# Separate PSUM banks in gate/up, and ScalarE reading queries, keys and diagonal blocks beside the inverse

## The chip, the cores and the metric

The kernel runs on one core of a Trainium2 chip. The metric is the device time of one execution in microseconds (us), the median of several runs. The engines are named as in the profile: PE is TensorE's matmuls and PEld its weight loads, DVE is VectorE, ACT is ScalarE, POOL is GpSimd; SPq and ACTq are the DMA issues in the queues of SyncE and ScalarE.

## The reference, cut to what matters

One layer of a decoder over 1024 tokens of 1024 features, all in float32. A combined projection feeds two groups of four heads: a gated delta rule in chunks of 64 tokens and a differential attention. Their outputs go through one output projection, and then through a SwiGLU block with 2816 hidden features. The parts that the change touches:

```python
# gated delta rule, per head and chunk of 64 tokens
L = jnp.where(strict, jnp.einsum('nbhcd,nbhsd->nbhcs', k_beta, k) * decay, 0.0)
A = L + jnp.eye(CHUNK, dtype=f32)
sol = lax.linalg.triangular_solve(A, rhs, left_side=True, lower=True, unit_diagonal=True)
q = l2norm(q.astype(f32)) * (Dk ** -0.5)
...
# the feed-forward block
gate, up = jnp.split(h @ w_gate_up[l], 2, axis=-1)
x = x + (jax.nn.silu(gate) * up) @ w_down[l]
```

## The kernel before

**Numbers.** A float32 product is made of three matmuls in a rounded 32-bit format: each operand is split into a high part (suffix `_h`) and the remainder (`_l`), and high x high, low x high and high x low are summed in PSUM (`mm3`, L144 to L146). So every projection result that is used again as an operand has to be read out of PSUM as a high part and a low part.

**PSUM.** All eight banks are taken: two tiles `big` of two banks each, two tiles `sm` and two tiles `fl` of one bank each. A dependency is tracked by tile: a matmul into one half of a `big` tile waits for every earlier instruction that reads the other half.

**Order.** A scheduler orders the instructions of each engine ahead of time; the program text gives it priorities and dependencies. Each engine then runs its own list in order, and a waiting instruction holds all that stand behind it, DMA issues included.

**The stage of the delta rule.** A loop over four heads (L463 to L486) makes keys and queries by projection, convolution and SiLU, sums their squares, and forms on PE the products K K^T and K Q^T in blocks of 128 tokens. DVE scales these with the decay into `At` (L482, tile `ak`) and `intra` (L485, tile `dec`). GpSimd then raises the sums of squares to a power (L489 `nk`, L490 `rqs`), and DVE scales `rqs` (L491), which is used only after the inverse. Then the diagonal 32x32 blocks of `At` are inverted: DVE transposes them with four instructions, one per group of 32 partitions, straight out of `At` (L502 to L504); 31 elimination steps of two small DVE instructions each follow (L506 to L511), and two more transposes (L514, L515). The products that go on from the inverse begin with L594 on PE.

**Beside the inverse** PE computes queries and keys of the attention's first two heads (`qk_dense`, in the order Q0, K0, Q1, K1; the halves n=0 and n=1 of the tokens share one `big` tile) and the value projections `v_dense`. For each half ACT writes the scaled high part out of PSUM (L535), and DVE reads PSUM again and subtracts it for the low part (L536). These parts lie in tiles `cv`, of which there are four buffers, and are sent to DRAM by DMAs issued on ACT's queue (L544, L545 for queries; L547, L548 for keys). The weights of the next projection are split by ACT (L151, the high part) and DVE (L153, the low part) or GpSimd (L157).

**The gate/up stage.** `gate_up(f)` runs for f = 1 to 21 (f = 0 is written out by itself, L1289 to L1321) and makes one 128-feature slice of gate and up for all tokens by a Strassen-like scheme: seven products of 12 matmuls each (`product`, L1200), in the order A11, S2, S3, S1, A12, S4, A22. `banks()` gives it four accumulators: `pa` is a tile `sm`, `pb` a tile `fl`, and `pc` and `pd` are the two halves of one `big` tile. S3 and A22 accumulate in `pc`, S1 and S4 in `pd`. DVE adds partial results (L1213) straight out of PSUM after each product: `u3` out of `pc` after S3, `tu` out of `pd` after S1, `tg` out of `pd` after S4, `tu` out of `pc` after A22. Between them DVE also forms the sums of raw weights for a later slice (L1168) and low parts (L1105). Raw gate and up weights come by DMA on SyncE's queue (L1156, L1158). The down projection follows.

Of the kernel before, what the change touches and what calls it, by code (L numbers as in the profile page):

```python
# [16 lines left out]
P = 128  # L17
# [51 lines left out]
def decoder_kernel(ctx: ExitStack, tc: tile.TileContext, a: dict, out: bass.AP):  # L69
# [392 lines left out]

    for h in range(H):  # L463
# [9 lines left out]
        for half in range(2):  # L473
            kk = sm()
            kq = sm()
            for jj in range(4):
                js = slice((half * 4 + jj) * P, (half * 4 + jj + 1) * P)
                nc.tensor.matmul(kk[:, jj * P:(jj + 1) * P], lhsT=KT[h][:, js], rhs=KT[h][:, js], start=True, stop=True)
                nc.tensor.matmul(kq[:, jj * P:(jj + 1) * P], lhsT=KT[h][:, js], rhs=QT[h][:, js], start=True, stop=True)
            b0 = h * 8 + half * 4  # L480
            for jj in range(4):
                nc.vector.scalar_tensor_tensor(out=At[:, b0 + jj, :], in0=kk[:, jj * P:(jj + 1) * P],  # L482
                                               scalar=brk_f[:, b0 + jj:b0 + jj + 1], in1=dec[:, b0 + jj, :],
                                               op0=ALU.mult, op1=ALU.mult)
            nc.vector.tensor_tensor(out=dec[:, b0:b0 + 4, :], in0=kq.rearrange("p (a b) -> p a b", a=4),  # L485
                                    in1=dec[:, b0:b0 + 4, :], op=ALU.mult)  # L486
    intra = dec
# [3 lines left out]
    nc.vector.tensor_scalar(out=rqs, in0=rqs, scalar1=DK ** -0.5, scalar2=None, op0=ALU.mult)  # L491
# [10 lines left out]
    for q in range(4):  # L502
        qs = slice(32 * q, 32 * q + 32)
        nc.vector.transpose(out=B[qs], in_=At[qs, :, qs].rearrange("s h c -> s c h"))  # L504
# [12 lines left out]
    def qk_dense(h, is_q, ps_of, mid=None):  # L517
# [6 lines left out]
        for n in range(2):  # L524
# [9 lines left out]
            if h < 2:  # L534
                nc.scalar.mul(out=sh[:, ns], in_=ps, mul=scale)  # L535
                nc.vector.scalar_tensor_tensor(out=sl[:, ns], in0=ps, scalar=scale, in1=sh[:, ns].bitcast(F32),  # L536
                                               op0=ALU.mult, op1=ALU.subtract)
                continue
# [79 lines left out]
    for h in range(H):  # L618
        ut = sm()
        for j in range(NT):  # L620
# [3 lines left out]
                                scalar1=-1.0, scalar2=None, op0=ALU.mult)  # L624
    Ktok = gp.tile([P, NHJ, P], F32, name="ak", bufs=1)
# [577 lines left out]
    def banks():  # L1203
        y = big()
        return sma(), flr(), y[:, 0:512], y[:, 512:1024]
# [83 lines left out]
    pa, pb, pc, pd = banks()  # L1289
# [143 lines left out]
```

## Time and profile before

| what | us |
|---|---|
| runs (three) | 1363.31, 1364.12, 1366.2 |
| median | 1364.12 |
| the profiled execution | 1363.61 |
| its span in the trace | 1361.5 |
| PE busy | 1298.3 |
| DVE busy | 766.1 |
| ACT busy | 484.7 |
| POOL busy | 240.6 |

The span is that of one profiled execution, from its first to its last recorded instruction; the time of that execution is about 2 us longer. Busy times count how long an engine executed something; a busy PE can still be slower than its best, when the clock granted to it is low. Waiting instructions show idle time before them, with what released them.

### The profile page before, as it was taken

Reading aid. Unit: us, or ns where it says so; the run is one execution under the profiler, and the core shown is the slowest. Engines: PE = TensorE matmul, PEld = TensorE weight load, DVE = VectorE, ACT = ScalarE, POOL = GpSimd, SP = SyncE. Lnnn points to the kernel's source line nnn. Section 1 sums busy time; section 2 is a strip of 40 time slices with the busy share of each in tenths; the row PEclk is TensorE's granted clock in tenths of the full one; section 3 lists DMA queues with packets and bytes.
Section 4 is the critical chain, followed back from the end, with each engine's and each line's share of the span. In section 5 each row is a group of like instructions: output and inputs, shape, how many; then the busy total and the mean of one; then the engine's idle time right before and its main releaser. Section 6 shows DMA issues by size and latency. Waiting matters only on the chain.

```text
span 1361.5 us, 16980 instructions
## 1 busy us (share of the span) xinstructions
PE 1298.3 (95%) x6540; PEld 1078.0 (79%) x6540; DVE 766.1 (56%) x1286; ACT 484.7 (36%) x920; POOL 240.6 (18%) x195
## 2 busy tenths in 40 slices
PE   6999998899999998989889999999999999999997
PEld 6978886798988777877668777878787888888886
DVE  6515659634836675876875465545544546545325
ACT  5233321132725564654543332322332234112104
POOL 1010030200023331232321212121122114200003
PEclk9999998999999998999989999999999999999999
DMA  7321112301146466735322323222222147422003
GB/s 218 111 62 43 35 32 88 114 17 31 33 141 196 144 206 183 227 102 200 119 78 93 108 82 104 87 70 77 93 78 92 63 156 276 140 93 93 0 1 124
DMA packets 122424, 143.30 MB, mean 105 GB/s; under 512 B 13632, under 2 KB 90728, under 8 KB 122344
## 3 DMA queue, kind: packets, MB, share of 16 engines
q1 hardware_dynamic: 114432, 128.07, 30.1%
q10 hardware_dynamic: 7912, 14.16, 2.8%
q8 instruction: 51, 0.84, 0.2%
q14 instruction: 29, 0.24, 0.1%
HBM read 103.40 MB, written 38.80 MB: 104 GB/s over the span
## 4 chain that ended last, share of the span: by engine, by line
PE 72%; DVE 12%; DMA 5%; issue 4%; ACT 4%; POOL 2%; SPq 1%; POOLq 0%; DVEq 0%; ACTq 0%
PE big L1200 17%; PE sm L1200 8%; PE big L144 4%; PE big L146 4%; PE big L145 4%; PE fl L144 4%; PE fl L146 4%; PE fl L145 4%; PE fl L1200 4%; PE sm L144 3%; PE sm L145 3%; PE sm L146 3%; PE sm L984 1%; DVE tmp L509 1%; DVE av L511 1%
## 5 line engine op out<-in xcount | busy, mean ns | idle before, releaser
L144 PE MATMUL big<-xT_h,w_h 128*128 128x512 f32 x320 | 128.2, 401 | 10.7 <-DVE cv L536 10.0
L146 PE MATMUL big<-xT_h,w_l 128*128 128x512 f32 x320 | 126.5, 395 | 0.0
L145 PE MATMUL big<-xT_l,w_h 128*128 128x512 f32 x320 | 126.1, 394 | 0.0
L1213 DVE TENSOR_TENSOR av<-big,av 128x512 f32<-128x512 f32 x88 | 60.5, 689 | 107.9 <-PE big L1200 107.8
L1200 PE MATMUL big<-hT_h,cv 128*128 128x512 f32 x264 | 90.8, 405 | 2.3 <-DVE av L1213 2.3
L1200 PE MATMUL big<-hT_h,avl 128*128 128x512 f32 x264 | 89.3, 399 | 1.2 <-DVE av L1213 1.2
L144 PEld LDWEIGHTS big<-xT_h,w_h 128*128 128x128 f32 x320 | 60.6, 190 | 26.0 <-DVE cv L536 12.3
L151 ACT CAST w_h<-w_raw 128x1024 fp32r<-128x1024 f32 x32 | 33.5, 1052 | 124.6 <-PE big L145 103.2
L146 PEld LDWEIGHTS big<-xT_h,w_l 128*128 128x128 f32 x320 | 60.5, 189 | 13.1 <-DVE w_l L153 0.7
L145 PEld LDWEIGHTS big<-xT_l,w_h 128*128 128x128 f32 x320 | 60.6, 189 | 11.8 <-issue 0.2
L1200 PEld LDWEIGHTS big<-hT_h,cv 128*128 128x128 f32 x264 | 50.4, 191 | 20.2 <-DVE av L1213 9.8
L1200 PEld LDWEIGHTS big<-hT_h,avl 128*128 128x128 f32 x264 | 49.5, 188 | 18.3 <-DVE av L1213 8.1
L1200 PE MATMUL sm<-hB_h,avl 128*128 128x512 f32 x176 | 59.0, 397 | 1.1 <-ACT hB_h L1130 1.1
L157 POOL TENSOR_TENSOR w_l<-w_raw,w_h 128x512 fp32r<-128x512 f32 x28 | 37.8, 1371 | 124.5 <-ACT w_h L151 123.3
L1213 DVE TENSOR_TENSOR x<-fl,x 128x512 f32<-128x512 f32 x48 | 32.9, 686 | 46.1 <-PE fl L146 46.1
L1213 DVE TENSOR_TENSOR x<-sm,x 128x512 f32<-128x512 f32 x48 | 33.0, 687 | 44.9 <-PE sm L146 44.1
L1200 PE MATMUL sm<-hB_h,cv 128*128 128x512 f32 x176 | 57.9, 389 | 0.0
L1168 DVE TENSOR_TENSOR xh<-w_raw 128x512 f32<-128x512 f32 x45 | 31.0, 688 | 46.8 <-DMA w_raw<-in_w_gate_up 46.8
L942 ACT ACTIVATE ae<-big,mx 128x128 f32<-128x128 f32 (+7 forms) x64 | 47.3, 741 | 27.9 <-DVE mx L933 11.8
L1105 POOL TENSOR_TENSOR avl<-xh,avl 128x512 fp32r<-128x512 f32 x23 | 30.7, 1335 | 148.4 <-ACT avl L1104 148.4
L1105 POOL TENSOR_TENSOR cv<-xh,cv 128x512 fp32r<-128x512 f32 x22 | 28.4, 1289 | 146.7 <-ACT cv L1104 146.7
L1200 PE MATMUL big<-hT_l,cv 128*128 128x512 f32 x132 | 52.6, 398 | 0.0
(431 smaller groups left out, 3480.8 us busy)
## 6 DMA issues: line engine op xcount, KB each, us to landing
w_raw<-in_w_gate_up SPq DMA_DIRECT2D x44, 512.0 KB, 4.0
w_raw<-in_w_in SPq DMA_DIRECT2D x24, 512.0 KB, 4.0
act<-av SPq DMA_DIRECT2D x22, 512.0 KB, 2.6
w_raw<-act SPq DMA_DIRECT2D x22, 512.0 KB, 4.3
cv<-in_w_down SPq DMA_DIRECT2D x20, 512.0 KB, 4.0
xt<-in_x SPq DMA_DIRECT2D x8, 512.0 KB, 5.1
ks<-cv ACTq DMA_DIRECT2D x8, 512.0 KB, 13.7
aqh<-qh SPq DMA_DIRECT2D x16, 256.0 KB, 5.6
```

Source lines behind the costliest of these rows:

```text
L144: nc.tensor.matmul(ps, lhsT=lh, rhs=rh, start=start, stop=False)
L145: nc.tensor.matmul(ps, lhsT=lh, rhs=rl, start=False, stop=False)
L146: nc.tensor.matmul(ps, lhsT=ll, rhs=rh, start=False, stop=stop)
L151: nc.scalar.copy(out=h, in_=raw)
L157: eng.tensor_tensor(out=l[:, c], in0=raw[:, c], in1=h[:, c].bitcast(F32), op=ALU.subtract)
L509: nc.vector.tensor_tensor(out=tv, in0=B[:, i + 1:, i:i + 1].broadcast_to([P, nr, ncol]), in1=X[:, i:i + 1, :ncol].broadcast_to([P, nr, nco ...
L511: nc.vector.tensor_tensor(out=X[:, i + 1:, :ncol], in0=X[:, i + 1:, :ncol], in1=tv, op=ALU.subtract)
L942: nc.scalar.activation(out=e[:, :n].rearrange("p (b c) -> p b c", b=nb), in_=s[:, :, :w], func=AF.Exp, bias=mx[:, m:m + 1], accum_out=zs[: ...
L1105: eng.tensor_tensor(out=l, in0=raw, in1=h.bitcast(F32), op=ALU.subtract)
L1168: nc.vector.tensor_tensor(out=r, in0=a0, in1=a1, op=alu)
L1200: nc.tensor.matmul(ps, lhsT=x[:, k, :], rhs=y[:, k, :], start=begin and k == 0 and n == 0, stop=k == HALF - 1 and n == 2, skip_group_check ...
L1213: nc.vector.tensor_tensor(out=out, in0=in0, in1=in1, op=ALU.add)
```

## The change

It has four parts. `banks()` gives `pc` and `pd` a `big` tile each, of which only the first bank is used; f = 0 keeps one `big` tile for both. In the loop over heads, after `At` has been written for half a head, ACT copies its diagonal blocks, four copies of 32 x 128 elements, into a new tile `diag`, and one transpose of all of it replaces the four transposes out of `At`. In `qk_dense` for the first two heads, ACT writes the scaled result out of PSUM twice, once rounded and once whole, and DVE subtracts the two in SBUF once for both halves. The scaling of `rqs` moves in the text from before the inverse to after it. From there on the lines of the changed kernel have numbers 1 to 3 higher.

```diff
--- before.py
+++ after.py
@@ -460,6 +460,7 @@
             nc.vector.tensor_reduce(out=dst[:, hh, half * 4:half * 4 + 4],
                                     in_=ps.rearrange("p (a b) -> p a b", a=4), axis=AX.X, op=ALU.add)
 
+    diag = op.tile([P, T], F32, name="av", bufs=4).rearrange("p (h c) -> p h c", c=32)
     for h in range(H):
         conv_silu(dense_T(C_K + h * P), 4 + h, KT[h])
         conv_silu(dense_T(C_Q + h * P), h, QT[h])
@@ -484,11 +485,13 @@
                                                op0=ALU.mult, op1=ALU.mult)
             nc.vector.tensor_tensor(out=dec[:, b0:b0 + 4, :], in0=kq.rearrange("p (a b) -> p a b", a=4),
                                     in1=dec[:, b0:b0 + 4, :], op=ALU.mult)
+            for q in range(4):
+                qs = slice(32 * q, 32 * q + 32)
+                nc.scalar.copy(out=diag[qs, b0:b0 + 4, :], in_=At[qs, b0:b0 + 4, qs])
     intra = dec
     fl = "p h t -> p (h t)"
     nc.gpsimd.tensor_tensor(out=nk.rearrange(fl), in0=ssk.rearrange(fl), in1=epow_pos, op=ALU.pow)
     nc.gpsimd.tensor_tensor(out=rqs.rearrange(fl), in0=ssq.rearrange(fl), in1=epow_neg, op=ALU.pow)
-    nc.vector.tensor_scalar(out=rqs, in0=rqs, scalar1=DK ** -0.5, scalar2=None, op0=ALU.mult)
     nc.vector.tensor_tensor(out=bup_f, in0=brk_f, in1=eGlG, op=ALU.mult)
 
 
@@ -499,9 +502,7 @@
     X = bx("X").rearrange("p (c s) -> p c s", s=32)
     nc.vector.memset(X, 0.0)
     nc.vector.memset(X.rearrange("p c s -> p (c s)")[:, 0::33], 1.0)
-    for q in range(4):
-        qs = slice(32 * q, 32 * q + 32)
-        nc.vector.transpose(out=B[qs], in_=At[qs, :, qs].rearrange("s h c -> s c h"))
+    nc.vector.transpose(out=B, in_=diag.rearrange("p h c -> p c h"))
     tmp = gp.tile([P, 256], F32, name="tmp", bufs=1)
     for i in range(31):
         nr, ncol = 31 - i, i + 1
@@ -533,8 +534,9 @@
             scale = DH ** -0.5 if is_q else 1.0
             if h < 2:
                 nc.scalar.mul(out=sh[:, ns], in_=ps, mul=scale)
-                nc.vector.scalar_tensor_tensor(out=sl[:, ns], in0=ps, scalar=scale, in1=sh[:, ns].bitcast(F32),
-                                               op0=ALU.mult, op1=ALU.subtract)
+                nc.scalar.mul(out=sl[:, ns].bitcast(F32), in_=ps, mul=scale)
+                if n == 1:
+                    nc.vector.tensor_tensor(out=sl, in0=sl.bitcast(F32), in1=sh.bitcast(F32), op=ALU.subtract)
                 continue
             nc.scalar.mul(out=sl[:, ns].bitcast(F32), in_=ps, mul=scale)
             nc.scalar.copy(out=sh[:, ns], in_=sl[:, ns].bitcast(F32))
@@ -622,6 +624,7 @@
                              start=True, stop=True)
         nc.vector.tensor_scalar(out=TT[h][0:64, :, 64:128], in0=ut[0:64].rearrange("p (j c) -> p j c", c=64),
                                 scalar1=-1.0, scalar2=None, op0=ALU.mult)
+    nc.vector.tensor_scalar(out=rqs, in0=rqs, scalar1=DK ** -0.5, scalar2=None, op0=ALU.mult)
     Ktok = gp.tile([P, NHJ, P], F32, name="ak", bufs=1)
     for h in range(H):
         Kh = Ktok[:, h * 8:h * 8 + 8, :]
@@ -1201,8 +1204,7 @@
                                  stop=k == HALF - 1 and n == 2, skip_group_check=not begin)
 
     def banks():
-        y = big()
-        return sma(), flr(), y[:, 0:512], y[:, 512:1024]
+        return sma(), flr(), big()[:, 0:512], big()[:, 0:512]
 
     def temps():
         return [op.tile([P, T], F32, name="av", bufs=4) for _ in range(3)]
@@ -1286,7 +1288,8 @@
         W0["A12"] = w_split(a12, nc.vector)
         W0["A22"] = w_split(a22, nc.vector)
 
-    pa, pb, pc, pd = banks()
+    pa, pb, both = sma(), flr(), big()
+    pc, pd = both[:, 0:512], both[:, 512:1024]
     tx, tg, tu = temps()
     u2, u3 = tx[:, n0], tx[:, n1]
     product(pc, W0["S3"], T3, True)
```

The scheduler makes new orders of it. On PE, in a call of `gate_up`, these rows stand before at the end of product S3 and the start of S1 (`big_7548` is the shared tile of `pc` and `pd`, `sm_7549` is `pa`, `hT3`, `hT1` and `hB1` are the activations of S3, S1 and A12):

```order
L1200 MATMUL big_7548<-hT3_l_5528,cv_7524 128x512
L1200 MATMUL big_7548<-hT3_h_5527,cv_7524 128x512
L1200 MATMUL sm_7549<-hB1_h_5519,cv_7541 128x512 [waits Activation_49]
L1200 MATMUL sm_7549<-hB1_l_5520,cv_7541 128x512
L1200 MATMUL sm_7549<-hB1_h_5519,cv_7541 128x512 [waits DVE_49]
L1200 MATMUL sm_7549<-hB1_h_5519,cv_7541 128x512
L1200 MATMUL big_7548<-hT1_h_5523,cv_7455 128x512 [waits DVE_49]
L1200 MATMUL big_7548<-hT1_l_5524,cv_7455 128x512
L1200 MATMUL big_7548<-hT1_h_5523,cv_7455 128x512 x2
```

And these stand there in the changed kernel (`big_7595` is `pc`, `big_7596` is `pd`, `sm_7593` is `pa`):

```order
L1203 MATMUL big_7595<-hT3_l_5562,cv_7569 128x512
L1203 MATMUL big_7595<-hT3_h_5561,cv_7569 128x512
L1203 MATMUL big_7596<-hT1_h_5557,cv_7500 128x512 [waits DVE_49]
...
L1203 MATMUL big_7596<-hT1_l_5558,cv_7500 128x512
L1203 MATMUL big_7596<-hT1_h_5557,cv_7500 128x512
L1203 MATMUL sm_7593<-hB1_h_5553,cv_7586 128x512 [waits Activation_49]
```

Four matmuls of A12 stood between S3 and S1, and now S1 follows S3 and is followed by A12. The same holds of the three that stood between S4 and A22.

On DVE, from the last head's blocks to the inverse, these rows stand before (`fl` holds K K^T, `sm` holds K Q^T, `cv_1747` is the low part of Q0):

```order
L482 SCALAR_TENSOR_TENSOR ak_923<-fl_1630,brk_919,dec_866 128x128 [waits PE_49,Pool_49]
L482 SCALAR_TENSOR_TENSOR ak_923<-fl_1630,brk_919,dec_866 128x128 x3
L491 TENSOR_SCALAR rqs_921<-rqs_921 128x32 [waits Pool_49]
L485 TENSOR_TENSOR dec_866<-sm_1631,dec_866 128x512 [waits DVE_49,PE_49]
L482 SCALAR_TENSOR_TENSOR ak_923<-fl_1645,brk_919,dec_866 128x128 [waits PE_49]
L482 SCALAR_TENSOR_TENSOR ak_923<-fl_1645,brk_919,dec_866 128x128 x3
L485 TENSOR_TENSOR dec_866<-sm_1646,dec_866 128x512 [waits DVE_49,PE_49]
L504 STREAM_TRANSPOSE av_1664<-ak_923 32x1024 x4
L536 SCALAR_TENSOR_TENSOR cv_1747<-big_1739,cv_1746 128x512 [waits Activation_49]
```

And these in the changed kernel (`av_924` is `diag`, `cv_1776` the low part of Q0):

```order
L483 SCALAR_TENSOR_TENSOR ak_923<-fl_1655,brk_919,dec_866 128x128 [waits PE_49,Pool_49]
L483 SCALAR_TENSOR_TENSOR ak_923<-fl_1655,brk_919,dec_866 128x128 x3
L627 TENSOR_SCALAR rqs_921<-rqs_921 128x32 [waits Pool_49]
L486 TENSOR_TENSOR dec_866<-sm_1656,dec_866 128x512 [waits DVE_49,PE_49]
L483 SCALAR_TENSOR_TENSOR ak_923<-fl_1674,brk_919,dec_866 128x128 [waits PE_49]
L483 SCALAR_TENSOR_TENSOR ak_923<-fl_1674,brk_919,dec_866 128x128 x3
L486 TENSOR_TENSOR dec_866<-sm_1675,dec_866 128x512 [waits DVE_49,PE_49]
L505 STREAM_TRANSPOSE av_1696<-av_924 128x1024 [waits Activation_49]
...
L512 TENSOR_TENSOR av_1697<-av_1697,tmp_1701 128x28x4 [waits DVE_49]
L153 TENSOR_TENSOR w_l_1900<-w_raw_1897,w_h_1899 128x1024 [waits DMAHW1_49,PE_49,Activation_49]
L510 TENSOR_TENSOR tmp_1701<-av_1696,av_1697 128x135 [waits DVE_49]
L539 TENSOR_TENSOR cv_1776<-cv_1776,cv_1775 128x1024 [waits Activation_49]
```

One transpose stands where four stood, behind a wait for ACT; the subtraction of Q0 stands behind four elimination steps and a weight split; the scaling of `rqs` has kept its place between the two halves of the last head, with its wait for GpSimd.

On ACT, these rows stand before, from the weight split for Q1 to the second half of K0 (`big_1739` is Q0, `big_1802` is K0):

```order
L151 CAST w_h_1868<-w_raw_1866 128x1024 [waits DMAHW1_49,PE_49]
L535 ACTIVATE cv_1746<-big_1739 128x512 [waits DVE_49,PE_49]
L544 DMA qh0_63<-cv_1746 128x1024 [waits Activation_49]
L545 DMA ql0_67<-cv_1747 128x1024 [waits DVE_49]
L535 ACTIVATE cv_1809<-big_1802 128x512 [waits PE_49]
L151 CAST w_h_1931<-w_raw_1929 128x1024 [waits DMAHW2_49,PE_49]
L535 ACTIVATE cv_1809<-big_1802 128x512 [waits DVE_49,PE_49]
```

And these in the changed kernel, from the second half of the last head's blocks on (`big_1832` is K0):

```order
L490 COPY av_924<-ak_923 32x128 [waits DVE_49]
L490 COPY av_924<-ak_923 32x128 x3
L151 CAST w_h_1899<-w_raw_1897 128x1024 [waits DMAHW1_49,PE_49]
L536 ACTIVATE cv_1775<-big_1768 128x512 [waits PE_49]
L537 ACTIVATE cv_1776<-big_1768 128x512
L546 DMA qh0_63<-cv_1775 128x1024 [waits Activation_49]
L547 DMA ql0_67<-cv_1776 128x1024 [waits DVE_49]
L536 ACTIVATE cv_1839<-big_1832 128x512 [waits PE_49]
L537 ACTIVATE cv_1840<-big_1832 128x512
L151 CAST w_h_1963<-w_raw_1961 128x1024 [waits DMAHW2_49,PE_49]
L536 ACTIVATE cv_1839<-big_1832 128x512 [waits PE_49]
L537 ACTIVATE cv_1840<-big_1832 128x512
```

The copies of the diagonal blocks now stand ahead of the weight split, each read of a half is two instructions, and the DMA of Q0's low part still stands between the reads of Q0 and those of K0.

## Rows read from the trace of the kernel before

**Rows 1.** The page: its span, and the busy time of each engine.

```profile
span 1361.5 us, 16980 instructions
...
PE 1298.3 (95%) x6540; PEld 1078.0 (79%) x6540; DVE 766.1 (56%) x1286; ACT 484.7 (36%) x920; POOL 240.6 (18%) x195
```

**Rows 2.** Waits, PE, 190 to 330 us: total us, times, longest.

```profile
PE big L144 <- DVE cv L536: 10.0, 4, 6.3
```

**Rows 3.** Waits, 720 to 1117 us (gate/up), of PE's weight loads.

```profile
PEld big L1200 <- DVE av L1213: 15.9, 42, 1.7
```

**Rows 4.** Chain that ended last: start us, us, what; product S2 of four calls.

```profile
802.78 2.65 PE fl L1200 x12
...
824.37 2.72 PE fl L1200 x12
...
843.85 2.72 PE fl L1200 x12
...
863.35 2.72 PE fl L1200 x12
```

**Rows 5.** Timeline, one gate/up call, PEld, SPq and DVE: start us, us, what, [idle before].

```profile
850.07 0.19 PEld L1200 LDWEIGHTS big<-hT_h,cv 128*128 128x128 f32 x1 [0.30 <-DVE av L1213]
...
858.51 0.19 PEld L1200 LDWEIGHTS big<-hT_h,avl 128*128 128x128 f32 x1 [0.37 <-DVE av L1213]
...
856.89 0.37 SPq L1158 DMA_DIRECT2D w_raw<-in_w_gate_up  x1
...
861.49 0.69 DVE L1168 TENSOR_TENSOR xh<-w_raw 128x512 f32<-128x512 f32 x1 [3.03 <-DMA w_raw<-in_w_gate_up]
```

**Rows 6.** Timeline of POOL beside the inverse.

```profile
237.69 2.70 POOL L157 TENSOR_TENSOR w_l<-w_raw,w_h 128x512 fp32r<-128x512 f32 x2 [34.26 <-ACT w_h L151]
```

**Rows 7.** Timeline of DVE: first head's end, then the inverse's start.

```profile
121.31 1.22 DVE L153 TENSOR_TENSOR w_l<-w_raw,w_h 128x1024 fp32r<-128x1024 f32 x1 [2.46 <-ACT w_h L151]
...
203.46 0.18 DVE L491 TENSOR_SCALAR rqs<-rqs 128x32 f32<-128x32 f32 x1 [5.82 <-POOL rqs L490]
...
205.99 7.71 DVE L504 STREAM_TRANSPOSE av<-ak 32x1024 f32<-32x1024 f32 x4
...
214.45 1.22 DVE L153 TENSOR_TENSOR w_l<-w_raw,w_h 128x1024 fp32r<-128x1024 f32 x1
...
217.74 0.68 DVE L536 SCALAR_TENSOR_TENSOR cv<-big,cv 128x512 fp32r<-128x512 f32 x1
...
219.02 0.32 DVE L511 TENSOR_TENSOR av<-av,tmp 128x156 f32<-128x156 f32 x1
...
230.27 0.68 DVE L536 SCALAR_TENSOR_TENSOR cv<-big,cv 128x512 fp32r<-128x512 f32 x1
...
237.98 1.29 DVE L511 TENSOR_TENSOR av<-av,tmp 128x156 f32<-128x156 f32 x1
```

**Rows 8.** Timeline of ACT and its DMA queue.

```profile
120.23 1.05 ACT L151 CAST w_h<-w_raw 128x1024 fp32r<-128x1024 f32 x1 [6.13 <-PE big L145]
...
214.45 0.34 ACTq L545 DMA_DIRECT2D ql<-cv  x1
214.84 0.60 ACT L535 ACTIVATE cv<-big 128x512 fp32r<-128x512 f32 x1 [9.82 <-DVE tmp L509]
...
279.62 0.37 ACT L610 ACTIVATE av<-fl 32x256 f32<-32x256 f32 x1 [4.75 <-PE fl L606]
```

**Rows 9.** Timeline of PE, beside the inverse and after it.

```profile
207.81 0.39 PE L146 MATMUL big<-xT_h,w_l 128*128 128x512 f32 x1
...
218.48 0.80 PE L144 MATMUL big<-xT_h,w_h 128*128 128x512 f32 x1 [0.26 <-DVE cv L536]
...
270.57 1.67 PE L594 MATMUL fl<-av,ak 128*128 128x64 f32 x14
```

**Rows 10.** Windows: us, busy of PE, PEld, DVE, ACT, POOL, granted clock, DMA share, GB/s.

```profile
214.00:219.00 5.00, 4.24 (x8) 2.49 (x9) 4.71 (x14) 0.60 (x1) 0.00 (x0) 0.50 0.68 207
```

**Rows 11.** DMA issues, 227.6 to 227.9 us: K0's low part, KB, us to landing.

```profile
ks<-cv ACTq DMA_DIRECT2D x1, 512.0 KB, 13.7
```

## The prediction

> **What bounds the kernel now.** The page comes first: PE is busy 95% of the span, every other engine 56% or less [rows 1]. So the time changes only where PE stands still, or where its work does. Two stages that the change touches show this.
>
> Beside the inverse, the list of waits says that PE's matmuls stood still for 10.0 us in four waits for DVE's read of a query or key tile (L536), the longest 6.3 [rows 2]. DVE's timeline shows why: from 205.99 it does the four transposes, 7.71 us, and the reads of PSUM stand behind them in its list [rows 7]. PE ends K0's first half at 207.81 and goes on with the second at 218.48, with seven matmuls of Q1 in between [rows 9]; those ran at a granted clock of 0.50, the lower level of 1.2 GHz [rows 10], after the standstill.
>
> In gate/up the weight loads wait 42 times for DVE's adds [rows 3], twice in each of 21 calls. One call shows them: 0.30 us before S1 and 0.37 before A22 [rows 5], each time because DVE still reads the other half of the same `big` tile. Four matmuls stand between, which hide the rest. The chain gives the period: S2 begins at 843.85 and again at 863.35, so 19.50 us a call; S2's own 12 matmuls take 2.72 us in it [rows 4]. Seven such products are 19.04.
>
> **The change, part by part.**
>
> *Separate banks.* S1 after S3 and A22 after S4 then write a tile that nobody reads. S1 needs the release of S4's tile of the call before, S3 that of A22's; both adds end before (below). Each call falls from 19.50 to 19.04, 0.46 us less (the two waits are 0.67 together, but their records count part of the load that the next matmul hides; I take the period). That would be 21 x 0.46 = 9.7. One call of them, 802.78 to 824.37, takes 21.59 us [rows 4]: it is held by a late weight for DVE's add, and its banks' waits lie inside that delay, so I count 20 calls, **9.2 us**. Bounds: nothing, if PE meets another wait at once; 21 x 0.67 = 14.1, if the waits vanish in full.
>
> What is late next is the add out of `pc` after A22 (`tu`). It must end before the next S3, two products or 5.44 us after A22's end. On DVE it stands behind the sum of raw weights (L1168), which waits for the up-weight's DMA: issued at 856.89, DVE goes on at 861.49 [rows 5]. That buffer becomes free when the last parts of the weights are made, which the change moves little. With 4.6 us of landing, the add ends some 2.6 us after A22, so about 2.9 us are to spare.
>
> *The inverse's start.* The order leaves the scaling of `rqs` in its place, so DVE still waits 5.82 us for GpSimd until 203.46 [rows 7]. I count nothing for the moved line. The second half of the last head's blocks is then scaled by about 205.3, as before. New are four copies on ACT of 32 x 128 elements. The trace has no such copy; above is a 128x512 read at 0.60, below nothing, near a 32x256 one at 0.37 [rows 8]. By the slope of these two, 0.0009 us an element, I take 0.26 each, 1.0 together (0 to 2.4): 206.4. The transpose of 128x1024 is bounded by one and by all of the four now in its place, 1.93 to 7.71 [rows 7]; I take 1.93, since each of the four runs over the same 1024 elements on fewer partitions: 208.4. Four elimination steps follow, which take 2.1 now between L153's end (214.45 + 1.22) and 217.74 [rows 7]; with the first half step, 2.2: 210.6. Then L153 at 1.2 and half a step of 0.3: 212.1.
>
> *Reads by ACT.* DVE's subtraction of Q0 comes there. It is one instruction of 1024 elements; L153 has that form, 1.22 [rows 7]: 213.3. ACT meanwhile has done the weight split (1.05) and Q0's two reads by 208.7, but then its list holds the DMA issue of Q0's low part, which waits for that subtraction, and behind it K0's reads. The issue takes 0.34, two reads 0.60 each [rows 8], 1.1 with their overlap: PE goes on with K0's second half at **214.8** instead of 218.48, 3.7 earlier, having done six matmuls of Q1 instead of seven, so 3.5 net. But before, PE's clock recovered from 0.50 in the stretch 214 to 219 [rows 10]; after a standstill as long, I expect the same here, now under K0's matmuls: some 4.5 us at twice the spacing of 0.227, so 2.2 us less gain.
>
> Next DVE subtracts K0. From 217.74 to 230.27, 12.5 us, DVE did the steps between two such reads, with an L153 and one more read [rows 7]; without these 10.7 and, with the steps that I counted already, 10.1; adding L153 and the subtraction again, it ends near 226.3. Then K0's low part is sent, issued at 226.4 to 226.8 and landing 13.7 us later [rows 11], at 240.1 to 240.5. Its buffer is the one into which ACT must write K1's first half (before, DVE did that, much later). So PE gets K1's second half at about 240.8, and from there to the first product after the inverse the order has 114 matmuls: 114 x 0.227 = 25.8, so 266.6 instead of 270.57 [rows 9]. **4.0 us** are gained. Bounds: 6.1, if the clock stays and the DMA lands as early as PE asks; nothing, if ACT's queue keeps all of it.
>
> *At no cost.* The copies of the first three heads and the memsets of the inverse's tile, which the order moves into the first head, lie in idle time: ACT has 6.13 us idle at the end of the first head [rows 8], DVE 2.46 [rows 7]; the copies take 2 x 1.0 a head, the memsets about 1.0. Uncovered, that would be 4 us in all. The second read of the last heads' queries delays one SiLU by 0.5, inside DVE's wait for GpSimd.
>
> At one place a rule speaks against the change. Beside the weight split on POOL at 237.69 [rows 6], a DVE step took 1.29 us, against 0.32 for its like at 219.02 [rows 7]. The Trainium skill, "SBUF — State Buffer", section "Who interferes with whom", says that a DVE instruction with two SBUF inputs and a GpSimd instruction that reads SBUF exclude each other, while one with at most one SBUF input is left alone. The trace agrees on the first. The new subtraction has two SBUF inputs, L536 had one; by the rule each may lose up to about 1.3 us, and the sum would be 10.6 to 11.9 if the first two met POOL. They stand at 212 and 225, and POOL is idle for the 34.26 us before 237.69 [rows 6]; so the sum stays.
>
> **Sum.** 9.2 + 4.0 = 13.2. The profiled execution, 1363.6 us (span 1361.5), would be 1350.4. It lies 0.5 under the median of the runs, 1364.1; by the median 1350.9. I say **1350.8**.
>
> **The rivals.**
>
> *A: all of the stall goes.* If the subtractions hold nobody (DMA and clock kind), ACT's reads of K0 follow those of Q0 and end at 208.7 + 1.1 = 209.8, 2.0 after PE's stop. Of the 10.0 in [rows 2] PE regains 8.0: 9.2 + 8.0 = 17.2, so 1347. Against it: ACT's list in the order above puts a DVE wait ahead of K0's reads.
>
> *B: nothing of the stall goes.* The wait moves from DVE's read to ACT's, held by the DMA issue and then the landing: 1364.1 - 9.2 = 1355. For it: 13.7 us of landing [rows 11]; against it: PE is 3.5 ahead even so.
>
> *C: the banks bring nothing.* PE, freed of the two waits, could meet the weights' low parts or the release of the previous call's tiles. Then 1364.1 - 4.0 = 1360. Against it: in the chain these calls hold only PE's pieces [rows 4].
>
> *D: slower.* The add after A22 is late for S3. Its spare time is 2.9 us; each us beyond costs 21 us in all, since every call has it. To lose the 13.2, the up-weight must land 3.5 us later than now, 8.1 after its issue instead of 4.6; at 4.0 beyond it, 1.1 x 21 - 13.2 = 10 us slower, 1374. Against it: the DMA engines have no new work here.
>
> **How the numbers follow.** The forecast gets 0.70, A 0.10, B 0.10, C 0.05, D 0.05. The forecast's own range is 1348 to 1354, from the 4.0 between 1 and 6 and the 9.2 between 8 and 11. Taking in most of A and B gives **1346 to 1357**; C and D and the rest of A stay out. A measurement here tells some 0.2%, 2.7 us, from no change: faster is the forecast, A, B and C (which just passes, 4.0), less a little, 0.94; slower is D less a little, 0.04; same 0.02.
>
> **What would show it.** The period of S2 at 19.04, no waits of weight loads for L1213 (numbered 1215 or so) in gate/up; one transpose of about 2 us and copies near 0.26; DVE's wait for GpSimd still near 5.8; PE back at 214.8 behind ACT, with a clock near 0.5 there; a last wait of PE for ACT's read of K1 near 237 to 241; the first product after the inverse near 266.6. The prediction is wrong if the calls keep 19.5 with a new releaser, if the copies or the transpose cost several times what I take, or if PE's wait moves to ACT in full.

## The result, and the profile after

| | before | after |
|---|---|---|
| median of the runs, us | 1365.11 (4 runs, 1363.31 to 1366.2) | 1347.61 (4 runs, 1346.14 to 1350.42) |
| profiled execution, us | 1363.61 | 1350.42 |
| its span, us | 1361.5 | 1348.1 |

The ratio of the runs is 0.9876, with a 95% interval of 0.9855 to 0.9896: 17 us faster, between 14 and 20. The time lies in the predicted range of 1346 to 1357, 3.2 below the predicted value. The profiled execution fell from 1363.6 to 1350.4, which is the predicted sum; below it turns out that one term was too small and that losses nobody had forecast made up for it.

The page of the changed kernel, span and busy times, against [rows 1]:

```profile
span 1348.1 us, 17043 instructions
...
PE 1290.8 (96%) x6540; PEld 1082.6 (80%) x6540; DVE 763.7 (57%) x1279; ACT 497.8 (37%) x960; POOL 241.7 (18%) x195
```

PE has the same 6540 matmuls and less time, ScalarE 13 us more work, VectorE about as much as before.

The waits of PE from 190 to 330 us, against [rows 2]:

```profile
PE big L144 <- ACT cv L537: 3.6, 3, 1.9
PE big L146 <- DVE w_l L153: 2.7, 1, 2.7
PE big L144 <- DVE ssk L470: 0.7, 1, 0.7
```

The 10.0 us of waits for VectorE's read of PSUM are gone; 3.6 for ScalarE's second read and 2.7 for a weight's low part stand in their place. The timelines show why, first VectorE's, against [rows 7]:

```profile
203.86 0.18 DVE L627 TENSOR_SCALAR rqs<-rqs 128x32 f32<-128x32 f32 x1 [5.54 <-POOL rqs L494]
...
206.96 2.09 DVE L505 STREAM_TRANSPOSE av<-av 128x1024 f32<-128x1024 f32 x1 [0.49 <-ACT av L490]
...
211.16 1.22 DVE L153 TENSOR_TENSOR w_l<-w_raw,w_h 128x1024 fp32r<-128x1024 f32 x1
...
212.50 1.22 DVE L539 TENSOR_TENSOR cv<-cv 128x1024 fp32r<-128x1024 f32 x1
...
225.55 1.22 DVE L539 TENSOR_TENSOR cv<-cv 128x1024 fp32r<-128x1024 f32 x1
```

The wait for GpSimd is still there, 5.54 us; one transpose of 2.09 stands for 7.71. Then ScalarE and its DMA queue, against [rows 8]:

```profile
205.70 1.22 ACT L490 COPY av<-ak 32x128 f32<-32x128 f32 x4 [6.13 <-DVE ak L483]
...
213.75 0.34 ACTq L547 DMA_DIRECT2D ql<-cv  x1
214.14 0.60 ACT L536 ACTIVATE cv<-big 128x512 fp32r<-128x512 f32 x1 [5.16 <-DVE av L512]
...
226.80 0.32 ACTq L550 DMA_DIRECT2D ks<-cv  x1
...
240.70 0.60 ACT L537 ACTIVATE cv<-big 128x512 f32<-128x512 f32 x1 [0.77 <-DMA ks<-cv]
```

ScalarE stands 5.16 us before it can issue the DMA of Q0's low part and read K0, and at 240.70 its write of K1 waits for K0's DMA. PE, against [rows 9]:

```profile
212.43 0.50 PE L146 MATMUL big<-xT_h,w_l 128*128 128x512 f32 x1 [2.66 <-DVE w_l L153]
...
215.28 0.80 PE L144 MATMUL big<-xT_h,w_h 128*128 128x512 f32 x1 [1.33 <-ACT cv L537]
...
241.35 0.50 PE L144 MATMUL big<-xT_h,w_h 128*128 128x512 f32 x1 [1.86 <-ACT cv L537]
...
267.33 1.89 PE L596 MATMUL fl<-av,ak 128*128 128x64 f32 x16
```

The first product after the inverse starts at 267.33 instead of 270.57. The window from 214 to 219 us, against [rows 10], has the same granted clock of 0.50; the DMA of K0, against [rows 11], lands after 13.9:

```profile
214.00:219.00 5.00, 3.72 (x9) 2.95 (x10) 4.59 (x13) 1.09 (x2) 0.00 (x0) 0.50 0.59 199
```

```profile
ks<-cv ACTq DMA_DIRECT2D x1, 512.0 KB, 13.9
```

In gate/up, three S2 products of the chain that ended last, against [rows 4], and the waits of weight loads from 720 to 1117 us, against [rows 3]:

```profile
817.61 2.72 PE fl L1203 x12
...
836.65 2.72 PE fl L1203 x12
...
855.69 2.72 PE fl L1203 x12
```

```profile
PEld big L1203 <- DVE av L1215: 2.6, 2, 2.1
```

The period is 19.04 us, which is 7 x 2.72, and of 42 waits of weight loads two are left.

### The profile page after: what moved, and what is told of

Its sections match the earlier page's. It is cut to its first block, busy times and chain, and to the rows that moved or that the text cites. A ratio compares the mean times of both kernels' runs of the same rounds, so it can differ in the third digit from the quotient of the medians.

```text
span 1348.1 us, 17043 instructions
## 1 busy us (share of the span) xinstructions
PE 1290.8 (96%) x6540; PEld 1082.6 (80%) x6540; DVE 763.7 (57%) x1279; ACT 497.8 (37%) x960; POOL 241.7 (18%) x195
## 4 chain that ended last, share of the span: by engine, by line
PE 72%; DVE 10%; DMA 5%; ACT 5%; issue 5%; POOL 3%; SPq 0%; POOLq 0%; DVEq 0%; ACTq 0%
PE big L1203 16%; PE sm L1203 8%; PE big L144 5%; PE big L145 4%; PE big L146 4%; PE fl L1203 4%; PE fl L144 4%; PE fl L146 4%; PE fl L145 4%; PE sm L144 3%; PE sm L146 3%; PE sm L145 3%; DMA ks<-cv 1%; PE sm L987 1%; DVE ae L957 1%
## 5 line engine op out<-in xcount | busy, mean ns | idle before, releaser
L1203 PE MATMUL big<-hT_h,avl 128*128 128x512 f32 x264 | 86.1, 390 | 0.0
L1203 PE MATMUL big<-hT_h,cv 128*128 128x512 f32 x264 | 86.0, 389 | 0.0
L945 ACT ACTIVATE ae<-big,mx 128x128 f32<-128x128 f32 (+7 forms) x64 | 47.3, 741 | 29.3 <-DVE mx L936 11.9
L153 DVE TENSOR_TENSOR w_l<-w_raw,w_h 128x1024 fp32r<-128x1024 f32 x18 | 22.0, 1224 | 52.4 <-ACT w_h L151 29.1
## 6 DMA issues: line engine op xcount, KB each, us to landing
ks<-cv ACTq DMA_DIRECT2D x8, 512.0 KB, 13.9
```

Of the source, the lines that this page charges most:

```text
L153: nc.vector.tensor_tensor(out=l, in0=raw, in1=h.bitcast(F32), op=ALU.subtract)
L945: nc.scalar.activation(out=e[:, :n].rearrange("p (b c) -> p b c", b=nb), in_=s[:, :, :w], func=AF.Exp, bias=mx[:, m:m + 1], accum_out=zs[: ...
L1203: nc.tensor.matmul(ps, lhsT=x[:, k, :], rhs=y[:, k, :], start=begin and k == 0 and n == 0, stop=k == HALF - 1 and n == 2, skip_group_check ...
```

## The experiments

To compare stages, I take three stretches between fixed instructions of PE. The first goes from the last short wait ahead of the inverse (192.57 before, 192.96 after) to the first product after the inverse. The second goes from there to the first matmul of S4, the second product of f = 0 (673.45 and 671.73), the third from there to PE's last short wait in the down projection (1156.97 and 1143.50). The last two columns are the start of S2 in the second call less that in the first, and the usual period.

| kernel | runs, us | ratio to before (95%) | beside inverse | to gate/up | gate/up, down | first call | period |
|---|---|---|---|---|---|---|---|
| before | 1365.11 | | 78.00 | 402.88 | 483.52 | 23.48 | 19.50 |
| after | 1347.61 | 0.9876 (0.9855 to 0.9896) | 74.37 | 404.40 | 471.77 | 19.22 | 19.04 |
| e1 banks | 1351.03 | 0.9887 (0.9869 to 0.9905) | 78.26 | 402.88 | 470.09 | 19.58 | 19.04 |
| e2 reads | 1363.31 | 0.9985 (0.9972 to 0.9997) | 76.71 | 403.31 | 487.28 | 25.82 | 19.50 |
| e3 gather | 1365.57 | 1.0001 (0.9986 to 1.0015) | 78.56 | 402.37 | 483.40 | 23.49 | 19.50 |
| e4 all but banks | 1360.36 | 0.9960 (0.9945 to 0.9975) | 74.13 | 402.91 | 483.57 | 23.62 | 19.50 |
| e5 scale on GpSimd | 1339.61 | 0.9807 (0.9793 to 0.9820) | 66.54 | 408.36 | 469.56 | 19.57 | 19.04 |
| e6 issue by SyncE | 1346.37 | 0.9861 (0.9842 to 0.9880) | 75.97 | 403.57 | 469.81 | 19.55 | 19.04 |
| e8 two DMAs | 1340.24 | 0.9815 (0.9802 to 0.9828) | 73.36 | 397.04 | 470.47 | 19.28 | 19.04 |
| e9 these three | 1333.16 | 0.9760 (0.9743 to 0.9777) | 64.74 | 397.39 | 470.50 | 19.56 | 19.04 |
| e10 e5 and e8 | 1338.67 | 0.9815 (0.9792 to 0.9838) | 71.97 | 397.31 | 469.56 | 19.48 | 19.04 |
| e11 two DMAs, late heads | 1342.86 | 0.9845 (0.9822 to 0.9867) | 74.79 | 397.30 | 468.71 | 19.46 | 19.04 |
| e12 before, two DMAs | 1360.31 | 0.9980 (0.9966 to 0.9994) | 79.65 | 398.59 | 482.58 | 23.66 | 19.50 |

The runs are medians; each ratio is to runs of the kernel before on the same chip. The stretches are of one profiled execution each.

**e1, the banks alone.** The kernel before with these lines:

```diff
-        y = big()
-        return sma(), flr(), y[:, 0:512], y[:, 512:1024]
+        return sma(), flr(), big()[:, 0:512], big()[:, 0:512]
...
-    pa, pb, pc, pd = banks()
+    pa, pb, both = sma(), flr(), big()
+    pc, pd = both[:, 0:512], both[:, 512:1024]
```

> The kernel before with separate banks alone. Theory (each bank's release no longer waits for an add that reads the other half): all the gate/up gain of the full change stands here too, some 12.7 us from the first product S2 (f = 0) to the last one, of which 18 calls give 0.46 each (period 19.04 instead of 19.50), the first call 4.3 (23.48 to 19.2) and the late one 0.6; the run is near 1352. Rival (part of the gate/up gain came from work that arrived earlier out of the stages ahead): the first call keeps some 23.5 us and the run is near 1356. The waits of PE for reads of query and key tiles stay at 10.0 us.

Measured: 1351.03, period 19.04, first call 19.58; the whole gain of gate/up stands here (13.4 in the third stretch, against 11.8 in the changed kernel). The rival is out: nothing in the stages ahead is needed for it.

**e2, ScalarE's reads alone.** The kernel before with these lines:

```diff
-                nc.vector.scalar_tensor_tensor(out=sl[:, ns], in0=ps, scalar=scale, in1=sh[:, ns].bitcast(F32),
-                                               op0=ALU.mult, op1=ALU.subtract)
+                nc.scalar.mul(out=sl[:, ns].bitcast(F32), in_=ps, mul=scale)
+                if n == 1:
+                    nc.vector.tensor_tensor(out=sl, in0=sl.bitcast(F32), in1=sh.bitcast(F32), op=ALU.subtract)
```

> The kernel before, with ScalarE alone reading queries and keys from PSUM; the four transposes and the shared bank stay. Theory (what sets the end of this stage is the release of K1's first half: by VectorE behind the inverse before, by ScalarE behind the landing of K0's low part now): K0's second half begins near 216.5 instead of 218.5, K1's second half near 243.5 instead of 248.0, the first product after the inverse near 267.5 instead of 270.6, a run 2 to 3 us shorter. Rival (the gain comes from the four transposes made one): the first product after the inverse stays within 1 us of 270.6.

Measured: the first product at 269.87, the stretch 1.3 us shorter instead of 3.0; this profiled execution is among the longest of the twelve runs, whose ratio of 0.9985 is 2.0 us, with an interval of 0.4 to 3.8. The 3.0 expected was too high a price. ScalarE's queue and PE in this kernel:

```profile
244.15 0.33 ACTq L546 DMA_DIRECT2D ql<-cv  x1
244.57 0.60 ACT L535 ACTIVATE cv<-big 128x512 fp32r<-128x512 f32 x1 [4.54 <-DVE tmp L509]
```

```profile
216.87 0.79 PE L146 MATMUL big<-xT_h,w_l 128*128 128x512 f32 x1 [7.61 <-DVE w_l L153]
...
245.71 0.50 PE L144 MATMUL big<-xT_h,w_h 128*128 128x512 f32 x1 [1.40 <-ACT cv L536]
```

The order of this kernel puts the DMA of Q1's low part ahead of K1's reads on ScalarE. VectorE subtracts Q1 at 242.90, late because its inverse is late, so K1's reads wait 4.54 us for that issue. In the changed kernel the same DMA stands behind the first two reads of K1. The rival's number (within 1 us of 270.6) holds here, but e3 takes its reason away.

**e3, the gather alone.** The kernel before with the tile `diag`, these copies and one transpose:

```diff
+            for q in range(4):
+                qs = slice(32 * q, 32 * q + 32)
+                nc.scalar.copy(out=diag[qs, b0:b0 + 4, :], in_=At[qs, b0:b0 + 4, qs])
...
-        nc.vector.transpose(out=B[qs], in_=At[qs, :, qs].rearrange("s h c -> s c h"))
+    nc.vector.transpose(out=B, in_=diag.rearrange("p h c -> p c h"))
```

> The kernel before, with the diagonal blocks gathered by ScalarE and one transpose in place of four; VectorE still reads queries and keys. Theory (the release of K1's first half sets the end, and here it still stands behind the end of the inverse): the transpose falls from 7.7 to 2.1 us and K0's second half begins near 217, but K1's second half begins near 243.6 with some 117 matmuls left, so the first product after the inverse is near 270, within 1 us of before. Rival (the shorter transposes carry the gain): it is near 266.6, a run some 4 us shorter.

Measured: no gain, first product at 270.41, though the transpose takes 2.07 us and the inverse ends early. VectorE's and PE's timelines here:

```profile
237.16 1.96 DVE L516 STREAM_TRANSPOSE av<-av 128x1024 f32<-128x1024 f32 x1
238.97 1.91 DVE L517 STREAM_TRANSPOSE av<-av 128x1024 f32<-128x1024 f32 x1
240.73 1.27 DVE L538 SCALAR_TENSOR_TENSOR cv<-big,cv 128x512 fp32r<-128x512 f32 x2
```

```profile
241.46 0.50 PE L144 MATMUL big<-xT_h,w_h 128*128 128x512 f32 x1 [3.67 <-DVE cv L538]
```

VectorE's next two reads of PSUM (the x2 of L538) stand behind the two transposes at the inverse's end, and PE waits for the first of them. The kernel before had these two waits there:

```profile
241.21 0.50 PE L144 MATMUL big<-xT_h,w_h 128*128 128x512 f32 x1 [1.74 <-DVE cv L536]
...
248.00 0.50 PE L144 MATMUL big<-xT_h,w_h 128*128 128x512 f32 x1 [1.74 <-DVE cv L536]
```

The second wait is gone in e3. But 120 matmuls are left behind 241.46, as many as behind 241.21 before; PE comes to this point no earlier, and after 3.67 us of standstill the granted clock is 0.72 from 241 to 247 us, where it was 1.00 before. So the earlier end of the inverse gives nothing, and the rival is out.

**e4, all but the banks.** The changed kernel with the `banks()` of before.

> The changed kernel with the shared bank of before: ScalarE's reads, the gather and the moved scaling of rqs. Theory: the first product after the inverse at 267.2 as in the changed kernel, 3.3 us earlier than before; gate/up keeps a period of 19.50 and the first call its 23.5; the run is 1.5 to 3.5 us shorter than before, near 1362. Rival (the pieces of the change depend on each other across the stages): gate/up gains here too, and the run is below 1358.

Measured as the theory has it: 74.13 beside the inverse, 3.9 less than before, and nothing in gate/up. The reads and the gather together gain what neither gains alone (1.3 and -0.6 in the stretches; by the runs 5.5 together, against 2.0 and nothing). In the stretches the two halves of the whole change are 13.4 (the third of e1) and 3.9 (the first of e4), together the 17 that the whole change gains by its runs. By their runs e1 and e4 gain 15.4 and 5.5, together 21; the difference of 4 us is about what the three intervals leave open.

**e5, the scaling of `rqs` on GpSimd.** The changed kernel with this line behind the power, in place of the one on VectorE:

```diff
+    nc.gpsimd.tensor_scalar(out=rqs, in0=rqs, scalar1=DK ** -0.5, scalar2=None, op0=ALU.mult)
...
-    nc.vector.tensor_scalar(out=rqs, in0=rqs, scalar1=DK ** -0.5, scalar2=None, op0=ALU.mult)
```

> The changed kernel with the scaling of rqs done by GpSimd behind its own power, so that VectorE's list has no wait for it between the two halves of the last head. Theory (the inverse starts behind that wait, and the end is set by the landing of K0's low part, which moves with it): VectorE's wait of 5.5 us is gone, the transpose starts near 201.5 instead of 207, PE's stop after K0's first half nearly vanishes and its clock stays up; K1's second half begins near 236.6 instead of 241.4 with a wait of 4 us ahead of it, the first product after the inverse is near 262.6 instead of 267.3, and the run near 1343. Rival (the wait for GpSimd was covered, PE is held by its own work): less than 1.5 us.

Measured: 66.54 beside the inverse, 7.8 less than in the changed kernel where 4.7 were expected, because K0's low part left at 220.78 and landed after 12 us, PE waited 0.88 for K1, and the granted clock stayed at 1.00 (from 207 to 217 us). The run is 1339.61; its profiled execution lost some of that in the second stretch (last section). The wait for GpSimd was the largest thing left in this stage.

**e6, the low parts issued by SyncE.** The changed kernel with `nc.sync` for `ql_dr` and the second DMA of `ks_dr` of the first two heads.

> The changed kernel with the DMAs of the low parts of Q0, K0, Q1, K1 issued from SyncE's queue, so that no DMA issue in ScalarE's list waits for VectorE. Theory (ScalarE's queue costs 2 us at K0's second half, but the landing of K0's low part sets the end): K0's second half begins near 213.3 instead of 215.3, K1's second half stays near 241.4, the first product after the inverse stays within 0.7 us of 267.3 and the run within 1.5 us of the changed kernel. Rival (ScalarE's queue sets the end): the first product is 2 us earlier.

Measured: K0's second half no longer waits, but the first stretch is 75.97, 1.6 longer than in the changed kernel, outside of what either expected. PE and a window of this kernel:

```profile
239.60 0.79 PE L144 MATMUL big<-xT_h,w_h 128*128 128x512 f32 x1 [3.23 <-ACT cv L537]
```

```profile
239.00:246.00 7.00, 6.40 (x16) 5.06 (x17) 7.00 (x6) 0.55 (x1) 0.00 (x0) 0.54 0.21 82
```

PE came to K1 earlier and stood 3.23 us there instead of 1.86, until the same DMA landed; then the clock was 0.54 until 246 us, against 1.00 from 241 to 247 in the changed kernel. So the landing did set the end: issued by SyncE at 225.74, K0's low part still took 13.2 us. The longer standstill cost clock on top. The runs cannot tell the two kernels apart.

**e8, the keys' high part by two DMAs.** The changed kernel with these lines:

```diff
-            nc.scalar.dma_start(out=ks_dr[h].rearrange("(a d) t -> a d t", d=DH)[0::3], in_=sh.bitcast(F32))
+            nc.scalar.dma_start(out=ks_dr[h][0:DH, :], in_=sh[0:DH].bitcast(F32))
+            nc.scalar.dma_start(out=ks_dr[h][3 * DH:4 * DH, :], in_=sh[DH:2 * DH].bitcast(F32))
```

> The changed kernel with the high part of the keys sent by two DMAs of 64 x 1024 instead of one of 2 x 64 x 1024. Theory (that one DMA runs on few of the DMA engines and holds up the low part behind it): K0's low part lands in some 3 to 6 us instead of 13.9, and no read of K1 waits for it. But the order also moves Q1's low-part DMA ahead of K1's reads in ScalarE's list, where it waits for VectorE's subtraction after the inverse (near 244), so that K1's second half begins near 245.4 with 102 matmuls left and the first product after the inverse is near 268.5, 1 us later than in the changed kernel. Rival (the landing has another cause): 13 us again, waits for ks remain.

Measured: the mechanism is as expected, the sum is not. The DMA issues from 223 to 226.5 us, and for the changed kernel the DMA engines' busy tenths in 40 slices from 215 to 260 us:

```profile
ks<-cv ACTq DMA_DIRECT2D x2, 256.0 KB, 3.6
...
ks<-cv ACTq DMA_DIRECT2D x1, 512.0 KB, 5.2
```

```profile
DMA  9600000000698511111482881055000112798211
GB/s 399 255 0 0 0 0 0 0 0 22 135 300 300 218 52 53 53 49 50 162 359 68 221 264 48 4 222 244 0 0 15 36 36 49 237 363 314 82 50 57
```

In the changed kernel the two DMAs of K0 show a tail of five slices at some 50 GB/s with a tenth of the 16 engines busy, about two of them; the form with two DMAs lands in 3.6 and 5.2 us. The first stretch fell by 1.0 instead of rising by 1, and the second by 7 (6 against that of e4), which I had not expected at all: heads 2 and 3 send their keys by the same lines in the middle of the attention.

**e9, the three together.**

> The changed kernel with all three: scaling of rqs on GpSimd, low parts sent from SyncE's queue, the keys' high part by two DMAs. Theory (these three are what holds PE beside the inverse): PE has less than 1.5 us of waits between 195 and 262, K1's second half begins near 233, the first product after the inverse is near 259 instead of 267.3, and the run near 1340, of which the later stages may keep a part. Rival (another wait, VectorE's end of the inverse or a weight's landing, takes their place): the first product is not before 262.

Measured: 1333.16, the fastest of all, and 7 less than expected, because the stretch to gate/up kept all of the 7 us of e8; 64.74 beside the inverse. The window from 195 to 257 us, of this kernel and then of the changed one:

```profile
195.00:257.00 62.00, 62.00 (x291) 51.53 (x290) 53.78 (x95) 17.58 (x31) 17.80 (x9) 1.00 0.35 111
```

```profile
195.00:257.00 62.00, 55.75 (x250) 45.13 (x249) 49.89 (x93) 15.48 (x29) 15.28 (x6) 0.94 0.29 97
```

PE is busy for all of it at the full clock, with 291 matmuls in place of 250. The rival is out: nothing takes the place of the three waits in this window.

**e10, without SyncE's queue.** The kernel of e9 with the low parts issued by ScalarE again.

> The changed kernel with the scaling of rqs on GpSimd and the keys' high part by two DMAs; the low parts are again issued by ScalarE. Theory (with VectorE's wait gone and the keys landing in 4 us, ScalarE's wait for Q1's subtraction still stands ahead of K1's reads): the first product after the inverse is 1 to 3 us later than in the kernel with all three (64.7 us after the first late weight wait near 192.5), the run 1334 to 1337. Rival (the queue of ScalarE costs nothing once the inverse starts early): the same as with all three, 1333.

Measured: 1338.67, and 7.2 us more than e9 beside the inverse, both more than expected. PE in this kernel:

```profile
239.07 0.80 PE L144 MATMUL big<-xT_h,w_h 128*128 128x512 f32 x1 [4.33 <-ACT cv L538]
```

ScalarE's issue of Q1's low part at 237.49 stands ahead of K1's reads and waits for VectorE, as in e2. PE stands 4.33 us, and the clock from 239 to 246 us is 0.64. So an issue in ScalarE's queue that is worth nothing in e6 is worth 7 us once the other two waits are gone; the rival is out.

**e11, two DMAs for heads 2 and 3 alone.** The edit of e8 under `h >= 2`.

> The changed kernel with the keys' high part sent by two DMAs for heads 2 and 3 alone, whose keys are made during the attention. Theory (the 7 us that the form with two DMAs gave between the inverse and gate/up come from these two heads): the stretch from the first product after the inverse to gate/up is near 397 us instead of 403 to 404, the stage beside the inverse stays at 74.4, the run near 1341. Rival (the gain came from the shifted order or from heads 0 and 1): it stays above 401.

Measured as the theory has it: 397.30 in the second stretch, 74.79 in the first, the run 1342.86. From 270 to 672 us PE's waits for ScalarE's `ae` (L945, here L949) are 3.1 us with 1.1 as the longest, against 6.9 and 4.6 in the changed kernel, and the same 3.1 and 1.1 in e8; how the landing of the keys leads to these waits was not followed.

**e12, two DMAs in the kernel before.** The edit of e8 in the kernel before.

> The kernel before with the keys' high part sent by two DMAs and nothing else. Theory (before the change the release of K1's first half stood behind the inverse on VectorE, not behind the landing; the landing became the limit only with the change): the stage beside the inverse stays within 0.7 us of its 78.0, and only the later stretch gains, some 6 us, so 1359. Rival (the landing held this stage before too): the stage falls by 1.5 us or more.

Measured: the second stretch gains 4.3 instead of 6 (the run is 1360.31), and the first one gains nothing; it is even 1.65 longer, which the theory did not have (PE waits 3.25 at 243.59 for VectorE's read of PSUM at 242.85, in place of 1.74 at 241.21, and the clock from 243 to 249 us is 0.72). So before the change the landing was not what held this stage.

## Why the prediction was right, point by point

*Separate banks.* The period of 19.04 came out as worked out from [rows 4]. The term was still too small: 9.2 against 12.7 from the first S2 to the last in the two profiles (406.92 and 394.21 us). I counted 20 calls at 0.46 and the late one at nothing, and did not look at the first call. It took 23.48 us before, and these rows of its timelines, of the kernel before, say why:

```profile
707.05 0.69 DVE L1168 TENSOR_TENSOR xh<-w_raw 128x512 f32<-128x512 f32 x1 [2.00 <-DMA w_raw<-in_w_gate_up]
...
709.69 0.68 DVE L1213 TENSOR_TENSOR av<-big,av 128x512 f32<-128x512 f32 x1
```

```profile
710.43 0.50 PE L1200 MATMUL big<-hT_h,cv 128*128 128x512 f32 x1 [2.33 <-DVE av L1213]
```

The add out of `pc` after S3 was late, since VectorE waited for a weight's DMA and had sums to do, and S1 in the other half of the tile had to wait for it, 2.33 us. The clock fell behind this standstill, as the windows of the kernel before show (the last three numbers are the granted clock, the DMA share and GB/s):

```profile
710.40:713.00 2.60, 2.57 (x7) 2.06 (x8) 1.17 (x2) 0.62 (x1) 0.64 (x1) 0.58 0.00 0
713.00:716.00 3.00, 3.00 (x12) 2.40 (x11) 0.69 (x1) 0.62 (x1) 0.87 (x2) 0.80 0.00 0
```

By these two that is another 1.7 us (2.6 x 0.42 + 3.0 x 0.20, an estimate). With its own bank S1 does not wait, and the clock is 1.00 in both windows: 19.22, so 4.26 us in one call. This is what made the term of the banks too small: this wait cost its own length and the clock behind it, while behind the 1.74 at 241.21 before and the 1.86 at 241.35 after the change the clock stayed at 1.00. The late call of [rows 4] gave 0.62 (20.97), where I counted nothing; but this call takes 19.83 in e4 and 19.50 in e3 with the shared bank, so the 0.62 is not shown to be the change's. One call still takes 19.46. The add that I feared would be late for S3 (rival D) never was in the usual calls.

*The inverse's start.* The wait of 5.8 us for GpSimd stayed (5.54), as the order said, in spite of the moved line. The copies took 0.30 each (0.26 taken), the transpose 2.09 (1.93). The whole stage began 0.39 later in this execution (192.96 against 192.57).

*Reads by ACT.* PE back with K0 at 215.28 (214.8 forecast), the clock 0.50 there, K0's subtraction done at 226.8 (226.3), the DMA issued at 226.80 and landing after 13.9 (13.7), K1's second half at 241.35 (240.8), the first product at 267.33 (266.6): each step within 0.8 us, most of it those 0.39. One of these agreements is partly luck: the terms that are written out for the end of K0's subtraction (213.3 + 10.1, an L153 and the subtraction) make 225.8, not the 226.3 that the forecast goes on with. The gain beside the inverse is 3.6 between the fixed instructions, against 4.0. That both edits are needed for it is what e2 to e4 add. The reading of the 10.0 us of [rows 2] was too simple: of the four waits only those of 6.28 and 0.26 stand behind the four transposes, the other two are the 1.74 at 241.21 and at 248.00 (e3).

*At no cost.* This held as far as the runs show: the short wait ahead of the inverse begins between 191.85 and 193.49 in the nine kernels with the copies, and between 192.57 and 193.16 in the four without.

*VectorE and GpSimd in SBUF.* All four subtractions took 1.21 to 1.22 us, so none met POOL's split, as the sum supposed. By the rule of the Trainium skill named there ("SBUF — State Buffer", "Who interferes with whom") another instruction with two SBUF inputs would; the trace agrees: one of L585, at 249.01, took 1.80 instead of 0.68, beside a split on POOL from 248.04 to 251.96.

*The sum.* The profiled execution gained 3.6 beside the inverse and 11.8 in the third stretch (12.7, less a slower f = 0: 18.07 to its S2 instead of 16.81, with 17.1 in e1 and 16.95 in e4), and lost 1.5 in the second stretch and 0.5 outside of the three: 13.4. That the profiled execution met the 13.2 of the forecast is luck: a term that was too small met losses that I had not forecast. That of the second stretch is probably this execution's and not the change's: e4 has the same instructions there and took 402.91, and of the four runs the profiled one is the longest. By the runs the gain is 17 us.

*The rivals.* A (all of the stall goes) gave 1347, and the median of 1347.6 lies there, but not by A's way: beside the inverse 3.6 us were gained and not 8.0, and the rest is gate/up. That all of the stall can go is what e9 shows, but only with three further edits. B and C are out by the rows above. D did not come.

## What to carry to other kernels

Two halves of one PSUM tile are one dependency here. It cost the usual 0.46 us a round, some 8 us in all, and 4.3 us more in the one round in which the other half's reader was late and the clock fell behind the wait, so look at the worst round too. When two engines' queues can hold the same release, moving one of them gains little; walk each queue, DMA issues included, up to the last release before the stage's end, since here two edits gained 1.3 and -0.6 alone and 3.9 together. And moving a line in the text moves nothing when the scheduler puts it back: the wait that it was about was still there, and was worth 8 us.

## What the runs showed of the hardware that was not expected

One DMA of 2 x 64 x 1024 held up the plain one issued 2 us after it: both landed after 13.9 us, with about two of 16 engines busy in the tail. The two need not stand in one engine's queue for it: in e6 SyncE issued the plain one, and it landed after 13.2 us. With the first one sent as two DMAs of 64 x 1024, these land in 3.6 us and the plain one in 5.2, worth some 7 us of the changed kernel's run with all four heads (e8) and 5 with two (e11). The Trainium skill, "DMA: Bandwidth & Descriptors", section "Rules for kernel authors", says that an outermost dimension smaller than 16 confines the whole DMA to at most as many engines; the tail agrees, about two.

The granted clock also fell while PE had no wait at all. In e5's profiled execution, among the small products after the inverse, the windows from 268 to 280 us read:

```profile
268.00:272.00 4.00, 4.00 (x29) 3.82 (x29) 0.83 (x2) 0.37 (x1) 0.00 (x0) 0.54 0.00 0
272.00:276.00 4.00, 4.00 (x15) 3.56 (x15) 0.00 (x0) 1.97 (x4) 0.00 (x0) 0.50 0.00 0
276.00:280.00 4.00, 4.00 (x29) 3.15 (x27) 0.83 (x2) 0.53 (x2) 0.00 (x0) 0.68 0.02 4
```

PE is busy in every one of them, and its last wait, 0.88 us, lies at 233.49; yet the granted clock is 0.50 to 0.68, in the middle one the lower level of 1.2 GHz. The changed kernel kept 1.00 through the same products (272 to 308 us). The three windows lose some 5 us by it (an estimate: 4 us each, by what the clock lacks to 1.00); the second stretch of e5's execution is 4 to 6 us longer than that of the other kernels with one DMA for the keys' high part, and its run of 1344.14 lies 4 to 5 us above the other four (1338.70 to 1339.99). What decides it in one execution and not in another was not tried.
